# Keeping TensorE's instructions of the three mixers in the order of the kernel's own planner

## The chip, the cores and the metric

The kernel runs on one core of one Trainium2 chip. The metric is the device time of one execution in microseconds (us). The kernel before takes 2852.42 us, the median of 3 runs (2849.89 to 2853.02).

## The reference

Two transformer-like blocks run one after the other on one sequence of 512 positions and 1024 channels, in float32. `x` is `(1, 512, 1024)`.

```python
for l in range(2):                                   # first block
    x = x + 0.5 * swiglu(rmsnorm(x, ffn1_norm[l]), ffn1_w_gu[l], ffn1_w_down[l])
    x = x + hybrid_mixing(rmsnorm(x, mix_norm[l]), w_in[l], ...)
    x = x + 0.5 * swiglu(rmsnorm(x, ffn2_norm[l]), ffn2_w_gu[l], ffn2_w_down[l])
h = rmsnorm(x, final_norm)
u = rmsnorm_2(h, norm_mix)                           # second block
p = u @ w_in
merged = gates[0] * (dilated_mixture_attention(p) @ w_a) \
       + gates[1] * (rwkv7_time_mix(p) @ w_r) + gates[2] * (s5_glu(p) @ w_s)
h = h + merged @ w_out
h = h + swiglu_2(rmsnorm_2(h, norm_ffn), w_gate_up, w_down)
return rmsnorm_2(h, norm_final)
```

`hybrid_mixing` projects its input by `w_in`, runs three branches on slices of the result (latent attention with 6 heads, a moving-average pool, attention with forget gates with 6 heads) and projects their concatenation by `w_out`. The hidden width of each SwiGLU is 2816.

## The kernel before

**Stages.** The program is one straight line: FFN, mixer 1 (layer 0), FFN, FFN, mixer 1 (layer 1), FFN, mixer 2, FFN, last norm. Activations lie feature by position: `x` is eight tiles of 128 channels x 512 positions. Each float32 product is computed from operands that are split into a high and a low part (ScalarE casts the high part, VectorE subtracts for the low one), as three matmuls into one PSUM bank: high x high, high x low, low x high. These are lines L201, L202 and L203 in `mm3`, called a triple here. A projection of 1024 channels to 128 outputs is eight triples, one for each of the eight k, and is called an item.

**The FFNs** are written by plain loops. The last loop of an FFN updates `x[o]` for o = 0 to 7 and calls `after(o)`, which makes the next stage's operand `xin[o]` from `x[o]` (L254, L255) and adds the squares of `x[o]` to `ssum` (L265, L266).

**The mixers** (`mix1` for the first block, `mix2` for the second) are written by a planner, class `Sched`. Every branch is a Python generator, a stream, that yields requests such as `("P", 0.64)` (0.64 us of TensorE), `V6` (0.62 us of VectorE), a wait for an event, or a place in a pool of tiles ("A" and "B" are PSUM, four banks each). The planner keeps a clock for each engine. At every step it finds the engine that can start first, takes among that engine's requests those that can start within `near` of it, picks the one with the lowest priority number, and lets its stream write its instruction into the program. The projections are one stream, `gemm_stream`, with priority 50, the filler: it asks for one triple at a time. Everything else has a lower number and goes first.

At a mixer's start the planner's clocks are set by `FV, FA, FG = 3.0, 2.2, 3.6` (VectorE, ScalarE, GpSimd are free so many us after TensorE), and the norm's stream `prep_end_s`, of priority 0, is ready at `D3` or `D4` = 5.2. Its first instruction is the matmul of `ones` with `ssum` at L285 (in `mix2` a second norm follows, whose matmul of `ones` with `ssum2` is L910). The row scale `rb`, which every evacuation of an item waits for, comes out of that stream. The weights of an item are cast by `load_w` (L393 on ScalarE, 0.97 us in the planner, L395 on VectorE, 1.135 us). The planner of `mix1` has `near` = 0.1 (`N1`) and an event lag of 0.2 (`E1`), that of `mix2` 0.5 (`N2`) and 0.4 (`E2`).

```python
first = min(self.active, key=lambda s: (start(s), s.prio))
t, e = start(first), first.req[0]
near = [x for x in self.active if x.req[0] == e and start(x) <= t + self.near]
s = min(near, key=lambda x: (x.prio + self.load * switch(x), start(x)))
```

`mix2` runs the planner in three parts: "a" (state-space branch, dilated attention, first preparation of the RWKV branch), "u" (RWKV: twelve units, at most four at a time, L1188 to L1341), "g" (gates, merge, `w_out`).

**The order that runs.** The planner decides only the order in which instructions are written. The library's scheduler then works through the whole program with a timing model of its own and may issue, on each engine, a later-written instruction ahead of an earlier one whose inputs its model does not have ready yet; among those that are ready the earlier-written one goes first. `keep_in_program_order` takes that freedom from one instruction: it is put behind the instruction written before it on its engine. The class `InOrder` wraps an engine so that all its instructions are treated so. Before the change it is used for VectorE, ScalarE and GpSimd in `ssm_tables`, and for no TensorE instruction.

Of the kernel before, what the change touches and what calls it, by code (L numbers as in the profile page):

```python
# [42 lines left out]
class Ev:  # L43


    def __init__(self, n=1):
        self.n, self.t, self.waiting = n, 0.0, []
# [7 lines left out]
class Sched:  # L55
# [64 lines left out]
    def run(self, group=0):  # L120
        start = lambda s: max(self.free[s.req[0]], s.ready)
        switch = lambda s: len(s.req) > 3 and s.req[3] != self.table
        while self.live[group]:
            assert self.active, "streams that wait for ever"
# [4 lines that stand above are left out]
            t, dur = start(s), s.req[1]  # L129
            if switch(s):  # L130
                self.table, dur = s.req[3], dur + 1.3
                if self.table in SETS:
                    self.preload(SETS[self.table])
            self.active.remove(s)
            self.free[e] = t + dur
            s.ready = t if len(s.req) > 2 and s.req[2] else t + dur
            s.last = e
            self.step(s)
# [5 lines left out]
class InOrder:  # L144
# [4 lines left out]

    def __getattr__(self, name):  # L150
        return lambda *a, **k: self.tc.keep_in_program_order(getattr(self.engine, name)(*a, **k))


class Kern:
# [220 lines left out]
    def vec(self, name):  # L375
        a, n = self.cols[name]
        return self.vecs[:, a : a + n]
# [1596 lines left out]
    def run(self, cols):  # L1974
        self.cols = cols
        self.x = [None] * NK
        vec = self.vec
        prep = lambda name: lambda o: self.prep_tile(o, vec(name))
        self.consts()
        self.load_x(0, "xT")  # L1980
        w0 = self.wraw("f1gu0", 0, 1024, 4)
        self.load_x(1, "xT")
        self.prep_start()
        self.operands(0, vec("f1n0"))
        w0 = self.wsplit(w0, 1024, 4)
        for k in range(1, NK):
            if k > 1:
                self.load_x(k, "xT")
            self.operands(k, vec("f1n0"))
        first = w0, self.wload("f1gu0", 1, 1024)  # L1990
        self.ident = self.const(self.cp, "ident", (P, P))
        for k in range(NK):
            self.sq_acc(k, self.x[k])
        for l in range(2):
            self.ffn(f"f1gu{l}", f"f1da{l}", f"f1db{l}", 0.25, prep(f"mixn{l}"), None if l else first)
            if self.stop == f"f1_{l}":
                break
            self.mix1(l, prep(f"f2n{l}"))
            if self.stop == f"y{l}":
                break  # L2000
            if self.stop == f"m_{l}":
                break
            last = l == 1
            nxt = (lambda o: self.prep2_tile(o)) if last else prep("f1n1")
            self.ffn(f"f2gu{l}", f"f2da{l}", f"f2db{l}", 0.25, nxt, beside=self.ssm_tables if last else None)
            if self.stop == f"f2_{l}":
                break
        if self.stop and (self.stop[-1] in "01" or self.stop == "b1"):
            self.store_x()
            return  # L2010
        self.mix2(prep("normf2"))
        if self.stop in ("ya", "yr", "ys"):
            return
        if self.stop == "b2m":
            self.store_x()
            return
        self.ffn("f3gu", "f3da", "f3db", 0.5, self.last_tile)
        if self.stop == "b2f":
            self.store_x()
            return  # L2020
        self.last_norm()
# [196 lines left out]
```

## Time and profile before

| | |
|---|---|
| median of 3 runs | 2852.42 us (2849.89 to 2853.02) |
| the profiled execution | 2848.72 us |
| its span, first to last instruction | 2846.8 us |
| TensorE busy (PE) | 2794.3 us, 98% |
| VectorE, ScalarE, GpSimd busy | 58%, 37%, 16% |
| mean granted TensorE clock | 0.994 |

The profiled execution is one run of the program under the hardware profiler. Its own time is 1.9 us more than its span, and 3.7 us less than the median of the runs. PE is TensorE's matmuls; PEld is the loading of their stationary operands, which runs beside them. The ends of matmuls are modelled, so the distance between starts says more of a matmul's cost than its duration does. PEclk is the clock that TensorE was granted as a share of 2.4 GHz: 1.00 or 0.50.

### The profile page before, as it was taken

How to read it: one execution, taken by the hardware profiler on the slowest of the kernel's cores; microseconds unless marked ns; L12 is line 12 of the kernel's file. 1: busy time of each engine (PE TensorE's matmuls, PEld its weight loads, DVE VectorE, ACT ScalarE, POOL GpSimd, SP SyncE). 2: the span in 40 equal slices, each digit the busy share in tenths (PEclk: the TensorE clock that was granted, in tenths of full speed). 3: DMA queues.
4: the chain of work that ended last, by engine and by line, in shares of the span. 5: the costliest groups of instructions: out<-in, count | busy, mean ns of one | idle time of the engine just before them, and what ended most of it. 6: DMA issues, size and time to landing. Idle time of an engine off the chain costs nothing. (4 is left out here: it accounts for less than half of the span.)

```text
span 2846.8 us, 33464 instructions
## 1 busy us (share of the span) xinstructions
PE 2794.3 (98%) x13036; PEld 2221.2 (78%) x13036; DVE 1640.0 (58%) x2544; ACT 1045.9 (37%) x1625; POOL 451.4 (16%) x368
## 2 busy tenths in 40 slices
PE   8999999999999999999999999999999999999998
PEld 6888877688888888887667788886677878788886
DVE  6454566655445554456665755658776756464454
ACT  4222354532223422234454325362324544332223
POOL 2010111020001200012101101124332212210101
PEclk9999999999999999999999999999999999999999
DMA  3223331223232232324122223343232016322322
GB/s 135 96 95 98 104 113 58 69 95 99 98 96 92 95 103 93 100 93 131 54 64 100 97 97 126 104 159 108 77 107 68 34 46 225 104 96 96 97 96 82
DMA packets 92118, 277.45 MB, mean 97 GB/s; under 512 B 11960, under 2 KB 13368, under 8 KB 91960
## 3 DMA queue, kind: packets, MB, share of 16 engines
q1 hardware_dynamic: 91960, 275.32, 29.4%
q8 instruction: 102, 1.67, 0.3%
q14 instruction: 56, 0.46, 0.0%
HBM read 255.87 MB, written 19.40 MB: 97 GB/s over the span
## 5 line engine op out<-in xcount | busy, mean ns | idle before, releaser
L201 PE MATMUL A<-xin,whi 128*128 128x512 f32 x2368 | 943.5, 398 | 6.8 <-ACT whi L192 5.1
L202 PE MATMUL A<-xin,whi 128*128 128x512 f32 x2368 | 933.0, 394 | 1.9 <-DVE xin L255 1.8
L203 PE MATMUL A<-xin,wlo 128*128 128x512 f32 x2368 | 930.2, 393 | 3.6 <-DVE wlo L193 1.9
L192 ACT CAST whi<-wraw 128x1024 fp32r<-128x1024 f32 (+2 forms) x343 | 349.7, 1020 | 1027.0 <-issue 378.1
L193 DVE TENSOR_TENSOR wlo<-wraw,whi 128x1024 fp32r<-128x1024 f32 (+2 forms) x343 | 500.8, 1460 | 86.8 <-ACT whi L192 60.4
L201 PEld LDWEIGHTS A<-xin,whi 128*128 128x128 f32 x2368 | 447.8, 189 | 119.2 <-issue 23.4
L202 PEld LDWEIGHTS A<-xin,whi 128*128 128x128 f32 x2368 | 447.5, 189 | 99.4 <-DVE xin L255 6.1
L203 PEld LDWEIGHTS A<-xin,wlo 128*128 128x128 f32 x2368 | 447.6, 189 | 98.3 <-DVE wlo L193 3.1
L332 POOL TENSOR_TENSOR u<-u,g 128x512 f32<-128x512 f32 x110 | 157.2, 1429 | 1419.0 <-DVE u L330 1145.6
L202 PE MATMUL B<-hl,whi 128*128 128x512 f32 x880 | 343.4, 390 | 1.5 <-DVE hl L217 1.3
L203 PE MATMUL B<-hh,wlo 128*128 128x512 f32 x880 | 342.5, 389 | 0.0
L201 PE MATMUL B<-hh,whi 128*128 128x512 f32 x880 | 342.5, 389 | 0.0
L341 DVE SCALAR_TENSOR_TENSOR x<-B,x 128x512 f32<-128x512 f32 x120 | 83.0, 692 | 307.3 <-PE B L203 307.3
L330 DVE TENSOR_TENSOR u<-A,rb 128x512 f32<-128x512 f32 x110 | 76.0, 691 | 256.2 <-PE A L203 256.2
L393 ACT CAST whi<-wraw 128x1024 fp32r<-128x1024 f32 (+2 forms) x117 | 119.6, 1023 | 214.3 <-PE A L202 133.7
L202 PEld LDWEIGHTS B<-hl,whi 128*128 128x128 f32 x880 | 165.2, 188 | 38.9 <-DVE hl L217 4.9
L201 PEld LDWEIGHTS B<-hh,whi 128*128 128x128 f32 x880 | 165.2, 188 | 34.9
L203 PEld LDWEIGHTS B<-hh,wlo 128*128 128x128 f32 x880 | 165.2, 188 | 34.0
L395 DVE TENSOR_TENSOR wlo<-wraw,whi 128x1024 fp32r<-128x1024 f32 (+2 forms) x117 | 155.3, 1327 | 25.9 <-ACT whi L393 25.3
L326 DVE TENSOR_TENSOR g<-A,rb 128x512 f32<-128x512 f32 x110 | 75.9, 690 | 157.5 <-PE A L203 157.4
L266 POOL TENSOR_TENSOR ssum<-ssum,sq 128x512 f32<-128x512 f32 x54 | 88.7, 1642 | 384.4 <-ACT sq L265 377.6
L216 ACT CAST hh<-u 128x512 fp32r<-128x512 f32 x110 | 68.4, 622 | 159.7 <-POOL u L332 159.7
(462 smaller groups left out, 2816.7 us busy)
## 6 DMA issues: line engine op xcount, KB each, us to landing
wraw<-in_f2gu SPq DMA_DIRECT2D x88, 512.0 KB, 3.3
wraw<-in_f1gu SPq DMA_DIRECT2D x87, 512.0 KB, 3.3
wraw<-in_w_in SPq DMA_DIRECT2D x76, 512.0 KB, 3.4
wraw<-in_f3gu SPq DMA_DIRECT2D x44, 512.0 KB, 3.3
wraw<-in_f1db SPq DMA_DIRECT2D x32, 448.0 KB, 3.2
wraw<-in_f2db SPq DMA_DIRECT2D x32, 448.0 KB, 3.3
wraw<-in_w_out SPq DMA_DIRECT2D x24, 512.0 KB, 3.5
wraw<-in_f1da SPq DMA_DIRECT2D x16, 512.0 KB, 3.3
```

The costliest lines, as they stand in the source:

```text
L192: nc.scalar.copy(hi[:, b], raw[:, b])
L193: nc.vector.tensor_sub(lo[:, b], raw[:, b], hi[:, b])
L201: mm(ps, wh, xh, start=first, stop=False)
L202: mm(ps, wh, xl, start=False, stop=False)
L203: mm(ps, wl, xh, start=False, stop=last)
L266: (nc.vector if k == NK - 1 else nc.gpsimd).tensor_add(self.ssum, self.ssum, sq)
L326: nc.vector.tensor_mul(g, pg, rb)
L330: nc.vector.tensor_mul(u, pu, rb)
L332: nc.gpsimd.tensor_mul(u, u, g)
L341: nc.vector.scalar_tensor_tensor(self.x[o], ps, scale, self.x[o], ALU.mult, ALU.add)
L393: nc.scalar.copy(hi[:, :width], raw[:, :width])
L395: nc.vector.tensor_sub(lo[:, :width], raw[:, :width], hi[:, :width])
```

## The change

During each of the three mixers `self.nc` is replaced by an object whose `tensor` is TensorE wrapped in `InOrder`, and everything else is as it was. Every TensorE instruction that a mixer writes is thereby put behind the TensorE instruction written before it. No instruction is added, removed or altered. The other engines, the DMA queues, and TensorE in the FFNs keep the scheduler's freedom.

```diff
+class Ordered:
+
+
+    def __init__(self, tc):
+        self.nc, self.tensor = tc.nc, InOrder(tc, tc.nc.tensor)
+
+    def __getattr__(self, name):
+        return getattr(self.nc, name)
...
+            self.nc = Ordered(self.tc)
             self.mix1(l, prep(f"f2n{l}"))
+            self.nc = self.tc.nc
...
+        self.nc = Ordered(self.tc)
         self.mix2(prep("normf2"))
+        self.nc = self.tc.nc
```

## Rows read from the trace of the kernel before

**Rows 1.** The page's first line.
```profile
span 2846.8 us, 33464 instructions
```

**Rows 2.** Windows: length; busy (instructions) of PE, PEld, DVE, ACT, POOL; PEclk, DMA share, GB/s.
```profile
375.80:590.00 214.20, 206.81 (x1071) 149.01 (x1070) 138.46 (x367) 107.89 (x228) 26.85 (x28) 1.00 0.23 73
1318.60:1530.00 211.40, 204.03 (x1047) 146.67 (x1046) 135.74 (x364) 105.69 (x225) 24.91 (x27) 0.98 0.23 71
1906.90:2150.00 243.10, 237.56 (x991) 166.97 (x990) 185.75 (x307) 82.35 (x145) 77.65 (x61) 0.98 0.31 105
2150.00:2362.00 212.00, 205.73 (x1429) 162.82 (x1429) 140.58 (x303) 106.95 (x232) 44.08 (x64) 0.99 0.15 51
2362.00:2440.00 78.00, 74.88 (x321) 60.65 (x320) 50.18 (x60) 25.19 (x34) 26.71 (x16) 0.98 0.64 218
```

**Rows 3.** Waits of PE, whole span: line, releaser, total us, times, longest.
```profile
PE B L521 <- DVE s L515: 11.7, 10, 2.1
...
PE B L1258 <- DVE FT L1243: 2.9, 3, 2.1
```

**Rows 4.** Timeline, layer-0 mixer's start: start, us, engine, line, operation, [idle before].
```profile
375.60 0.39 PE L203 MATMUL B<-hh,wlo 128*128 128x512 f32 x1
375.83 0.39 PE L201 MATMUL A<-xin,whi 128*128 128x512 f32 x1
...
376.51 0.39 PE L201 MATMUL A<-xin,whi 128*128 128x512 f32 x1
...
379.64 0.68 DVE L266 TENSOR_TENSOR ssum<-ssum,sq 128x512 f32<-128x512 f32 x1
...
380.38 1.13 PE L285 MATMUL B<-ssum,ones 128*128 128x512 f32 x2
```

**Rows 5.** Timeline of PE, layer-1 mixer's start.
```profile
1318.60 0.39 PE L201 MATMUL A<-xin,whi 128*128 128x512 f32 x1
...
1323.15 0.70 PE L285 MATMUL B<-ssum,ones 128*128 128x512 f32 x1
```

**Rows 6.** Timeline of PE, start of mixer 2.
```profile
1906.93 0.39 PE L201 MATMUL A<-xin,whi 128*128 128x512 f32 x1
...
1911.48 1.13 PE L285 MATMUL B<-ssum,ones 128*128 128x512 f32 x2
...
1914.98 1.02 PE L910 MATMUL B<-ssum,ones 128*128 128x512 f32 x2
...
1930.58 0.39 PE L203 MATMUL A<-xin,wlo 128*128 128x512 f32 x1
1932.29 2.45 PE L1868 MATMUL B<-su,BT 32*128 32x512 f32 x4 [1.32 <-issue]
```

**Rows 7.** Windows around long waits; columns as in Rows 2, PEclk third from last.
```profile
1412.50:1414.70 2.20, 0.10 (x2) 0.06 (x1) 2.20 (x5) 0.48 (x1) 2.14 (x2) 1.00 0.25 15
1414.80:1418.20 3.40, 3.40 (x11) 2.36 (x12) 2.64 (x9) 1.93 (x5) 1.75 (x3) 0.50 0.36 145
1933.70:1940.40 6.70, 6.70 (x16) 4.48 (x15) 5.53 (x8) 0.63 (x1) 5.21 (x5) 0.50 0.28 91
...
2432.10:2435.30 3.20, 3.20 (x7) 2.28 (x8) 1.89 (x3) 1.62 (x2) 0.00 (x0) 0.50 0.17 64
...
470.40:474.00 3.60, 3.60 (x25) 2.50 (x26) 2.71 (x10) 2.05 (x5) 1.82 (x3) 1.00 0.34 125
```

**Rows 8.** Timeline: other matmuls inside a triple, first and last of 88.
```profile
491.59 0.62 PE L569 MATMUL B<-c_ident,w 128*128 128x128 f32 x4
...
505.56 0.39 PE L201 MATMUL A<-qn1h,whi 128*128 128x512 f32 x1
505.70 0.41 DVE L515 TENSOR_SCALAR s<-s,st 128x384 f32<-128x384 f32 x1
...
506.16 0.55 PE L521 MATMUL B<-c_ident,s 128*128 128x128 f32 x3 [0.21 <-DVE s L515]
...
2346.96 1.12 PE L1061 MATMUL B<-sq,c_bones 128*128 128x512 f32 x2
```

## The prediction

> **What bounds the kernel now.** I read the page first, then the windows by stage, then TensorE's waits, then the timeline at the places where those lead. The span is 2846.8 us [rows 1], and TensorE is the bound nearly everywhere: in the five windows that cover the mixers (layer 0, layer 1, and the parts "a", "u", "g" of mixer 2) the length minus PE's busy time is 7.39, 7.37, 5.54, 6.27 and 3.12 us, 29.7 us together [rows 2]. The reader should see that VectorE, the next busiest, has room in each of them. So the change can win at most those 29.7 us and the slow clock that follows some of them, and what it adds in TensorE waits is paid in full unless the same stage has idle time later that takes it up. The longest waits by line are those of the transposes L521 for VectorE's L515, 11.7 us in 10 waits over both layers, and of L1258 for L1243, 2.9 us in 3 [rows 3].
>
> **The change part by part.** It adds and removes no instruction. On the chip a matmul waits for the same operands as before; new is only what stands behind it. Where the scheduler used to let filler triples pass a matmul whose input was late, TensorE now stands still, and with it every triple behind. Nothing moves on SP's or POOL's queue by the edit itself. VectorE, ScalarE and GpSimd are left to the scheduler and have room [rows 2], so I cost their reordering at nothing; without that room the delay of an engine would come back as lateness of the matmuls that I count below.
>
> *The start of each first-block mixer.* In the planner the first item's weights are cast from 2.2 to 3.17 us on ScalarE and from 3.30 to 4.435 us on VectorE, so with the lag of 0.2 the first triple is taken at 4.635 and ends at 5.275. The norm's matmul L285 is ready at 5.2 and has priority 0: it comes second. The written order is one triple, L285, the rest. In the trace the first triple starts at 375.83, the second at 376.51 (a triple is 0.68 us), and L285 only at 380.38, right after VectorE's last sum of squares ends at 380.32 [rows 4]: six triples and a matmul were let past it, because the weights had in fact been cast during the FFN. Kept in order, TensorE stands from 376.51 to 380.38, 3.87 us. Layer 1 repeats it: 1318.60 + 0.68 = 1319.28 to 1323.15, 3.87 us [rows 5]. Nothing hides it, since L285 waits for the FFN's own last tile. It isn't won back by `rb` either, which comes no earlier; the items come later by so much, and the attention that uses up the mixer hangs on items. I take all of it, 2 x 3.87 = 7.7 us; the ends are nothing (the later idle 7.4 us takes it up) and 7.7.
>
> *The start of mixer 2.* The first triple could be taken at 4.835 (lag 0.4), but L285 at 5.2 lies within the 0.5 of `near` and wins: it is written ahead of every triple. The trace bears that out by the next matmul of that stream: the planner puts L910 at the first free place from 12.34 on, and L285's end at 6.06 plus ten triples of 0.64 is 12.46; in the trace thirty matmuls of the filler, ten whole triples, run from 1906.93 until L910 at 1914.98, nineteen of them ahead of L285 [rows 6]. So the order written is L285, ten triples, L910. Kept, TensorE stands from 1906.93 to 1911.48, 4.55 us. Part of it comes back: before, four items filled the four banks "A" by 1930.58 and TensorE then waited 1.32 us for `rb` [rows 6]; 4.55 us later that wait is gone. Net 4.55 - 1.32 = 3.2 us.
>
> *The clock.* After the wait of 2.1 us before 1414.6 the granted clock was 0.50, the 1.2 GHz level, for 3.4 us, and after the longest in the mixers for as long from 2432.1 on; in the stretch from 1933.7 it was 0.50 for 6.7 us; after a like wait of 2.1 us before 470.3 it stayed at 1.00 [rows 7]. A stretch of 3.4 us at half speed does 1.7 us of work, so it costs 1.7 us. The starts' waits are nearly twice as long as the one that slowed it, so I count 1.7 us for each first-block mixer, 3.4 us; for mixer 2 a slow stretch at the start stands against the 6.7 us that no longer follow a wait, and I count nothing. The Trainium skill (TensorE: Matmul & The Clock Gate, Part 1: The HAM clock gate) says that half speed is TensorE's default and that idleness sends it back there. By that alone each of the three starts would pay 1.7 us, 5.1 instead of 3.4; the stretch from 470.4 shows that not every wait of this size does.
>
> The starts sum to 7.7 + 3.2 + 3.4 = 14.3 us.
>
> *Inside the mixers.* Where a matmul of a branch stands between two matmuls of a triple, the scheduler has put it back: the planner never splits a triple, so it was written ahead of it. There are 88 such places beside the three L285, 10 in each first-block mixer, 22 in part "a" and 46 in part "u"; the first and the last of them stand in the rows [rows 8]. Kept in order, TensorE would wait where the triple began until the operand was there. At 505.56 a triple begins, L515 ends at 505.70 + 0.41 = 506.11, L521 starts at 506.16 after 0.21 us of idleness that was there already: 0.39 us more [rows 8]. The same difference, with 0.06 us from the writer's end to the matmul, over all 88 and with those ready in time at 0, sums to 2.6 + 2.6 + 5.6 + 11.0 = 21.7 us. Matmuls put back by whole triples stand on a boundary and don't show; if lateness is spread evenly over a triple, a third does, and the upper end is 1.5 x 21.7 = 32 us. The lower end is about 0: a wait for one branch lets the others' VectorE and ScalarE work catch up, so that the next is not late any more. I take half the upper end, 16 us, since several streams are in flight in every part.
>
> Sum: 14.3 + 16 = 30.3 us, 2848.7 + 30.3 = 2879 us for the profiled execution; the median of the runs lay 3.7 us above it, so 2883 us.
>
> **The rivals.** *Only the starts cost* (waits inside the mixers share one another's time, or fall into idleness that was there): 2852.4 + 14.3 = 2867 us. For it: 29.7 us of idle time are there to be filled [rows 2]. Against it: that idleness sits in a few long waits, and the 88 places are spread.
>
> *Lateness piles up* in part "u", where 46 of 87 passages from a triple to another matmul are inside a triple, so that its order is far from the written one. At one triple of 0.68 us for each of the 87 it costs 59 us: 2852.4 + 14.3 + 59 = 2926 us.
>
> *Faster: the scheduler's order is itself what causes the waits.* L521's waits of both layers (11.7 us) [rows 3] and all idle time of "a" and "u" (5.54 + 6.27 us) [rows 2] would go, and with them half of the slow stretches from 1414.8 and 1933.7 and of two like the former in mixer 2 (1.7 + 3.4 + 3.4 us) [rows 7]: 32 us. It decides from 14.3 us on, where the starts are paid; in full it gives 2852.4 + 14.3 - 32 = 2835 us. For it: some matmuls were issued some 2 us ahead of their operand, which a better plan would not do. Against it: the scheduler only lets later-written work pass, so the written order has that matmul no later relative to the triples that passed it.
>
> *No effect*: the written order is the one that already runs, 2852 us. Against it speak L910's ten triples.
>
> **How the numbers follow.** The forecast of 2883 us gets 0.38 (its own range 2868 to 2900: the starts with 0 to 32 us), only the starts 0.24, piling up 0.12, faster 0.17, no effect 0.09. The range is 2842 to 2926: below it lies most of the faster case, above it half of the piling up, under 0.2 together. A measurement of this kernel can tell about 0.2%, 5.7 us, from no change. Slower holds the first three, 0.74; the same holds no effect and a little of the faster case, 0.10; faster 0.16.
>
> **What would show it.** In the profile after, each first-block mixer begins with one triple, a PE wait of about 3.8 us for VectorE's `ssum`, then L285; mixer 2 begins with a wait of about 4.5 us and L285, and L910 follows ten triples later. PEclk shows 0.50 behind these. No triple has another matmul inside it, and PE's waits by line grow by many short ones for L515, L477, L482, L1243 and the copies at L441. The prediction is wrong if L285 still comes after several triples, if the windows of "a" and "u" are no longer than now, or if L521's waits shrink by more than the starts add.

## The result, and the profile after

The kernel with the change took 2903.16 us (median of 4 runs, 2902.27 to 2903.88), the kernel before on the same chip 2852.72 us (4 runs, 2849.89 to 2854.03). The ratio is 1.0182, with a 95% interval of 1.0168 to 1.0197: slower by 50.4 us. The forecast was slower, by 30.3 us.

The profiled execution took 2902.65 us against 2848.72, 53.9 us more. Lines in the mixers have moved by 10, and all their TensorE instructions now carry the line of the wrapper, L151; the triples of the FFNs are L211 to L213. The page's first line, and its busy times:

```profile
span 2900.9 us, 33474 instructions
...
PE 2812.7 (97%) x13036; PEld 2232.6 (77%) x13036; DVE 1645.9 (57%) x2544; ACT 1043.0 (36%) x1623; POOL 455.4 (16%) x368
```

TensorE runs the same 13036 instructions, is busy 18.4 us longer (2812.7 - 2794.3) and the span grew by 54.1: the rest is idle time. These are the windows of the same stages, with the columns of [rows 2]. Each ends behind the last wait of its stage; the counts of instructions show that the ends are not at the same instruction, so what can be compared is the idle time:

```profile
376.27:592.70 216.43, 200.80 (x1029) 144.30 (x1028) 134.60 (x361) 103.32 (x222) 23.71 (x26) 0.98 0.22 69
1331.10:1545.20 214.10, 198.86 (x1013) 142.04 (x1013) 132.94 (x360) 102.57 (x221) 21.94 (x25) 0.97 0.22 68
1930.20:2186.70 256.50, 242.82 (x995) 170.51 (x994) 187.26 (x309) 82.29 (x145) 81.74 (x61) 0.97 0.30 99
2186.70:2399.70 213.00, 196.36 (x1358) 153.29 (x1358) 137.27 (x295) 99.08 (x223) 42.35 (x64) 0.98 0.13 43
2399.70:2493.00 93.30, 89.97 (x385) 72.89 (x384) 55.90 (x66) 30.21 (x41) 26.73 (x16) 0.98 0.59 200
```

Length minus PE's busy time is 15.63, 15.24, 13.68, 16.64 and 3.33 us, 64.5 together, where [rows 2] gave 29.7. The stages before "g" gained 8.2, 7.9, 8.1 and 10.4 us of idle time, "g" 0.2. The first three hold a mixer's start each; without the waits there (3.70, 3.70 and 4.38 us, below) 4.5, 4.2 and 3.8 us are left, so inside the mixers "u", the stage with the most places in triples, lost by far the most.

Added up over all of TensorE's records, idleness grew by 35.6 us. In the mixers the granted clock was 0.50 in thirteen stretches of 3.4 us and one of 6.8 us, where before there were five and one: eight more, each worth 1.7 us, are 13.6 us of work not done. (At the end of the program it was low for 2.8 us longer, where TensorE has hardly any work.) 4.7 us is left over. These three make the 53.9. The mean granted clock is 0.989 in all four runs of the change; in the 19 runs of the kernel before beside e9 to e11 it is 0.993 to 0.997.

Whom TensorE waits for, over the whole span (columns as in [rows 3]):

```profile
PE B L151 <- DVE s L525: 14.2, 16, 2.1
PE B L151 <- DVE ssum L276: 11.8, 3, 4.4
PE B L151 <- DVE FT L1253: 10.7, 13, 3.1
...
PE A L151 <- ACT sT L451: 4.9, 12, 0.7
...
PE B L151 <- issue: 1.8, 1, 1.8
```

L525 is L515 of before, and L1253 is L1243. The waits for `s` grew from 11.7 us in 10 to 14.2 in 16, those for `FT` from 2.9 us in 3 (1.6 more in one by another matmul's line) to 10.7 in 13. New is the wait for `ssum`, 11.8 us in 3: the three starts, which answer to [rows 4 to 6]. Timeline of PE:

```profile
376.27 0.61 PE L151 MATMUL A<-xin,whi 128*128 128x512 f32 x2
376.73 0.39 PE L151 MATMUL A<-xin,wlo 128*128 128x512 f32 x1
380.82 2.07 PE L151 MATMUL B<-ssum,ones 128*128 128x512 f32 x2 [3.70 <-DVE ssum L276]
...
1331.61 0.39 PE L151 MATMUL A<-xin,wlo 128*128 128x512 f32 x1
1335.70 1.51 PE L151 MATMUL B<-ssum,ones 128*128 128x512 f32 x2 [3.70 <-DVE ssum L276]
...
1929.87 0.39 PE L213 MATMUL B<-hh,wlo 128*128 128x512 f32 x1
1934.63 2.08 PE L151 MATMUL B<-ssum,ones 128*128 128x512 f32 x2 [4.38 <-DVE ssum L276]
...
1945.22 1.02 PE L151 MATMUL B<-ssum,ones 128*128 128x512 f32 x2
...
1955.38 0.39 PE L151 MATMUL A<-xin,wlo 128*128 128x512 f32 x1
1957.56 0.66 PE L151 MATMUL B<-su,BT 32*128 32x512 f32 x1 [1.79 <-issue]
```

One triple, a wait of 3.70 us, the norm's matmul; in mixer 2 a wait of 4.38 us with no triple ahead, and the second norm's matmul after exactly thirty matmuls. The view counts a wait from the modelled end of the matmul before; by the distance of starts, as the forecast counted, less 0.23 us for that matmul, the three are 3.86, 3.86 and 4.53 us. In none of the 88 places of [rows 8] does another matmul stand inside a triple any more. The last two rows were not foreseen: the wait before the matmul on `su` was 1.32 us in [rows 6] and should have gone; it is 1.79 us.

The clock behind waits (columns as in [rows 7]): the start of layer 0, two places later in that mixer, the start of mixer 2, and part "g".

```profile
380.60:384.00 3.40, 3.18 (x6) 1.86 (x7) 0.85 (x2) 0.48 (x2) 0.00 (x0) 0.50 0.44 126
476.20:479.60 3.40, 3.40 (x16) 2.36 (x16) 2.43 (x10) 2.11 (x5) 1.50 (x3) 0.51 0.33 119
513.70:517.10 3.40, 3.15 (x9) 2.35 (x9) 2.10 (x6) 2.01 (x6) 0.00 (x0) 0.50 0.45 126
1933.60:1940.30 6.70, 5.67 (x11) 3.85 (x12) 2.43 (x5) 3.27 (x5) 0.00 (x0) 0.50 0.92 308
2486.70:2490.10 3.40, 3.40 (x10) 2.66 (x9) 2.39 (x3) 1.78 (x3) 0.00 (x0) 0.51 0.21 40
```

The first and the fourth are the starts (mixer 2 had a stretch as long before). The fifth was there before too. The second and third lie behind waits inside the mixers of 2.10 and 1.54 us. The second is not the change's alone: before, layer 1 had the like at 1414.8 [rows 7], and two of the runs below (e3, e9) that leave the layer-0 mixer as it was have it there. The third is new: it stands in both first-block mixers of the four traces in which these are kept in order with the planner's lag as it was (this one, e2, e6, e11), and in no other trace.

### The profile page after: what moved, and what is told of

Read it like the earlier page. It is cut to its first block, busy times and chain, and to the rows that moved or that the text cites. A ratio compares the mean times of both kernels' runs of the same rounds, so it can differ in the third digit from the quotient of the medians.

```text
span 2900.9 us, 33474 instructions
## 1 busy us (share of the span) xinstructions
PE 2812.7 (97%) x13036; PEld 2232.6 (77%) x13036; DVE 1645.9 (57%) x2544; ACT 1043.0 (36%) x1623; POOL 455.4 (16%) x368
## 5 line engine op out<-in xcount | busy, mean ns | idle before, releaser
L211 PE MATMUL A<-xin,whi 128*128 128x512 f32 x1760 | 688.4, 391 | 7.3 <-ACT whi L202 5.1
L212 PE MATMUL A<-xin,whi 128*128 128x512 f32 x1760 | 686.9, 390 | 2.1 <-DVE xin L265 2.0
L213 PE MATMUL A<-xin,wlo 128*128 128x512 f32 x1760 | 686.0, 390 | 1.9 <-DVE wlo L203 1.9
L151 PE MATMUL A<-xin,whi 128*128 128x512 f32 x1216 | 401.1, 411 | 0.0
L211 PEld LDWEIGHTS A<-xin,whi 128*128 128x128 f32 x1760 | 331.0, 188 | 77.3 <-ACT whi L202 5.1
L213 PEld LDWEIGHTS A<-xin,wlo 128*128 128x128 f32 x1760 | 331.0, 188 | 71.8 <-DVE wlo L203 3.1
L211 PE MATMUL B<-hh,whi 128*128 128x512 f32 x880 | 342.5, 389 | 0.0
L213 PE MATMUL B<-hh,wlo 128*128 128x512 f32 x880 | 342.4, 389 | 0.0
L151 PEld LDWEIGHTS A<-xin,whi 128*128 128x128 f32 x1216 | 225.1, 193 | 68.9 <-issue 28.8
L151 PE MATMUL A<-xin,wlo 128*128 128x512 f32 x608 | 241.3, 397 | 1.7 <-DVE wlo L405 1.7
L211 PEld LDWEIGHTS B<-hh,whi 128*128 128x128 f32 x880 | 165.1, 188 | 34.9
L213 PEld LDWEIGHTS B<-hh,wlo 128*128 128x128 f32 x880 | 165.2, 188 | 34.2
L405 DVE TENSOR_TENSOR wlo<-wraw,whi 128x1024 fp32r<-128x1024 f32 (+2 forms) x117 | 155.3, 1327 | 21.7 <-ACT whi L403 20.7
```

The costliest lines, as they stand in the source:

```text
L211: mm(ps, wh, xh, start=first, stop=False)
L212: mm(ps, wh, xl, start=False, stop=False)
L213: mm(ps, wl, xh, start=False, stop=last)
L405: nc.vector.tensor_sub(lo[:, :width], raw[:, :width], hi[:, :width])
```

## The experiments

All ratios are to the kernel before on the same chip. "Kept" means that TensorE's instructions are kept in the written order there; elsewhere the scheduler is free.

**e1: only the starts kept** (the first eight TensorE requests from L285 on; then the wrapper hands out the free engine).

```diff
     @property
     def tensor(self):
+        if self.left is not None:
+            self.left -= 1
+            self.on = self.left >= 0
+        return self.pin if self.on else self.nc.tensor
...
+            if nc.left is None:
+                nc.left = 8
```

> TensorE is kept in the planner's order only from each mixer's start until eight triples after the norm's matmul of ones and ssum; the rest of each mixer is left to the scheduler. Theory (the starts are paid in full, with the slow clock behind them): waits for ssum of 3.7 + 3.7 + 4.4 us, less 0.2 us that the kernel before waited there, and 1.7 us of slow clock at each first-block mixer, about 15 us: 2868 us. Rival (the later idle time of the mixers takes the starts' waits up): 2853 to 2858 us.

Measured 2869.19 us, ratio 1.0068 (1.0051 to 1.0085): 18.7 us more. The starts are paid in full, and the rival (2853 to 2858 us) falls; the forecast's 14.3 us lies just below the interval's lower end of 14.5. The same three waits stand in its trace:

```profile
PE B L151 <- DVE ssum L283: 11.8, 3, 4.4
```

**e2: all kept, and the planner counts no time for the casts of each mixer's first item.**

```diff
-    def load_w(self, name, idx, width, out):
+    def load_w(self, name, idx, width, out, cast=True):
...
-        yield ("A", 0.12 + width * 0.00083)
+        if cast:
+            yield ("A", 0.12 + width * 0.00083)
...
-                w = self.load_w(*items[i][:2], width(i), ws)
+                w = self.load_w(*items[i][:2], width(i), ws, i > 0)
```

> The changed kernel, but the planner counts no time for the cast of each mixer's first item, which in the traces is done during the FFN; so it writes eight triples ahead of the norm's matmul in the first-block mixers and seven in mixer 2. Theory: in the first-block mixers the wait for ssum and its slow clock go, 2 x (3.7 + 1.7) = 10.8 us; in mixer 2 the wait only moves from ssum to the next matmul that hangs on rb (the one that reads su), since as many triples stand ahead of that as in the changed kernel: 2892 us. Rival (all three starts are won back, about 15.5 us): 2888 us or less. Rival (the starts cost nothing net): 2903 us.

Measured 2890.61 us, ratio 1.0141 (1.0125 to 1.0156), as the theory had it. The plan now writes triples ahead of the norm's matmul, so none of the three starts waits for `ssum`. But in mixer 2 the time is given back at the next matmul of that chain, which waits for `rb` as before. Timeline of PE in mixer 2:

```profile
1916.23 0.61 PE L151 MATMUL A<-xin,whi 128*128 128x512 f32 x2
...
1920.99 1.02 PE L151 MATMUL B<-ssum,ones 128*128 128x512 f32 x2
...
1942.73 2.04 PE L151 MATMUL B<-su,BT 32*128 32x512 f32 x2 [8.28 <-issue]
```

4.38 + 1.79 = 6.2 us of waits became one of 8.28 us.

**e3: only part "u" kept** (the first-block mixers are not wrapped; in mixer 2 the wrapper starts switched off, and is on during the planner's run of "u").

```diff
...
+        nc.on = True
         sch.run("u")
+        nc.on = False
...
```

> TensorE is kept in the planner's order only in part u of mixer 2 (the RWKV units). Theory (lateness piles up): in the kernel before, the last matmuls of the units stand up to 69 filler matmuls later than written, 69 x 0.227 = 15.7 us; kept in order all of that is waited for: about 2869 us. Rival (the waits of one unit give time to the others, as half of the places inside triples, 11 us, had it): 2858 to 2861 us. Rival (the loss of mixer 2 comes from part a): 2853 us.

Measured 2868.06 us, ratio 1.0064 (1.0049 to 1.0079): 17.5 us more against the 15.7 us of the theory. That figure came from the order in which the two kernels' instructions are written and issued: at the end of "u" the scheduler had let 69 filler matmuls pass, 69 x 0.227 us. The put-back adds up over the stage and is paid in full. Not all of it shows as waits: from the start of "u" to the next FFN the trace is 18.4 us longer than before, of which 9.8 us are more idle time of TensorE and 3.4 us more slow clock; 5.2 us lie in neither.

**e4 and e5: the planner counts 0.5 us instead of 0.2 us from another engine's end to the TensorE instruction that uses its result**, with all kept (e4) and with nothing kept (e5).

```diff
-TO = dict(P=0.2, V=0.13, A=0.13, G=0.13)
+TO = dict(P=0.5, V=0.13, A=0.13, G=0.13)
```

> The changed kernel, but the planner counts 0.5 us instead of 0.2 us from another engine's end to a TensorE instruction that hangs on it. Theory (the waits inside the mixers come from matmuls written for the very moment at which the planner has their operand): most waits of 0.2 to 0.5 us go, about half of the 38 us lost inside the mixers, 2884 us (2878 to 2890). Rival (the waits come from few places where the plan is wrong by a microsecond or more, or from the order of the streams): 2898 to 2908 us.

Measured 2894.53 us, ratio 1.0159 (1.0144 to 1.0175), between the two theories. In its windows of "a" and "u" the idle time is 265.20 - 245.90 = 19.3 us (13.7 after the change alone) and 8.95 us (16.6):

```profile
1928.40:2193.60 265.20, 245.90 (x994) 172.21 (x994) 185.44 (x306) 83.22 (x148) 79.28 (x61) 0.95 0.29 96
2193.70:2401.50 207.80, 198.85 (x1391) 161.16 (x1391) 142.08 (x313) 99.19 (x212) 41.87 (x63) 0.98 0.14 48
```

"u" gained 7.7 us and "a" gave 5.6 of them back, with a clock of 0.95. The run told nothing clear of the cause, because it changed every plan; e9 to e11 repeat it for "u" alone.

> The kernel before (nothing kept in order) with the planner's 0.5 us instead of 0.2 us: what that constant does without the change, the control for the run with both. Theory (the gain of the run with both comes from fewer waits of kept matmuls): no gain here, 2850 to 2858 us. Rival (the constant makes the plan better for the whole kernel): 2842 to 2846 us, and what the run with both gained has nothing to do with the change.

Measured 2855.28 us, ratio 1.0022 (1.0012 to 1.0031). With the order free the lag wins nothing, it costs 5.5 us: e4's gain exists only where the written order binds.

**e6: all kept except the starts and "u".**

> TensorE is kept in the planner's order in the mixers except at their starts (until eight triples after the norm's matmul) and in part u of mixer 2. Theory (the parts add up): the changed kernel lost 50 us, the starts alone 19, part u alone 17, so 14 us are left for the attention of the first-block mixers and part a of mixer 2: 2866 us. Rival (waits at the start bring about the waits further in, by the slow clock or by weights that come late): 2853 to 2859 us. Rival (the parts take time from one another, and each alone costs more): 2872 us or more.

Measured 2873.08 us, ratio 1.0083 (1.0068 to 1.0098): 23.3 us, where the parts should have left 50.4 - 18.7 - 17.5 = 14.2. The theory of 2866 us falls, and the time lies where the last rival puts it, by which each part alone costs more. e1, e3 and e6 make 18.7 + 17.5 + 23.3 = 59.5 us, and all together 50.4. One row shows where a part is counted twice, the matmul on `su` again:

```profile
1943.04 2.04 PE L151 MATMUL B<-su,BT 32*128 32x512 f32 x2 [6.72 <-issue]
```

With the start free the triples that passed L285 are used up early, and the kept matmul on `su` waits 6.72 us, 4.9 more than the 1.79 with everything kept. 59.5 - 4.9 = 54.6 us; the 4 us that remain are within the three intervals (each 4 to 5 us to either side).

**e7: "u" with TensorE and VectorE kept.**

```diff
+        self.pinv = InOrder(tc, tc.nc.vector)
...
+    @property
+    def vector(self):
+        return self.pinv if self.on else self.nc.vector
```

> As the run with part u alone, and in that part VectorE too is kept in the planner's order; TensorE's order is the same to the instruction. Theory (TensorE waits in u because VectorE's instructions stand in another order than the plan's): most of the 10 us of new waits go, 2856 to 2861 us. Rival (they are in the plan's order or near it, and take longer than planned, such as those beside GpSimd): 2866 to 2880 us.

Measured 2864.66 us, ratio 1.0050 (1.0035 to 1.0065): between the two, and nearer to the rival. Idle time of "u" fell only from 214.70 - 198.84 = 15.86 us in e3 to 13.60:

```profile
2151.20:2359.80 208.60, 195.00 (x1358) 152.27 (x1358) 138.28 (x295) 99.41 (x223) 42.84 (x63) 0.99 0.13 44
```

VectorE's free order is at most a small part of the cause: 14.9 us against e3's 17.5, with intervals that overlap. My first explanation, that the results come late because the scheduler puts other work ahead of them on VectorE, falls as the main one. No run kept ScalarE's or GpSimd's order.

**e8: the plan of e2 with nothing kept.**

> The kernel before (nothing kept in order), but the planner counts no time for the cast of each mixer's first item. Theory (the scheduler makes good such errors of the plan, as it lets filler pass a late matmul): 2848 to 2856 us. Rival (a better plan helps it too): 2840 to 2846 us.

Measured 2848.45 us, ratio 0.9997 (0.9987 to 1.0006). The free scheduler makes such an error of the plan good by itself.

**e9 and e10: "u" alone kept, as in e3, with the lag of 0.5 us (e9) or 1.0 us (e10) in "u" alone.** The edit of e9, shown against e3:

```diff
...
         nc.on = True
+        TO["P"] = 0.5
         sch.run("u")
+        TO["P"] = 0.2
         nc.on = False
...
```

> Part "u" alone is kept in order, as in e3_u_only, and in that part alone the planner counts 0.5 us instead of 0.2 us from another engine's end to the TensorE instruction that uses its result. Theory (the written order is too optimistic about when VectorE's and ScalarE's results are there, so matmuls stand too early among the triples and TensorE waits): with 0.3 us more at each step most of the put-back is in the written order already; the idle time of "u" falls from 15.9 us towards the 9 us that e4_lag_half showed, and the time from 2868 us to 2858 us (2855 to 2862). Rival (the waits come from the order in which the other engines work, which a lag for TensorE does not touch): 2865 to 2870 us, idle time of "u" 13 us or more.

> The same with 1.0 us instead of 0.2 us, in part "u" alone. Theory (the plan is too optimistic): the idle time of "u" falls to the 6 to 7 us that it had with the order free, and the time to 2855 us (2851 to 2860), a little above the kernel before, since a branch then takes longer in the plan. Rival (the other engines' order): 2865 to 2870 us. A second rival (a lag that is too long makes the branches the bound of the plan, and the filler runs out): above 2870 us, with the idle time at the end of "u".

Measured 2855.31 us, ratio 1.0021 (1.0011 to 1.0031), and 2852.29 us, ratio 1.0009 (1.0000 to 1.0019). The cost of keeping "u" in order goes from 17.5 to 6.5 to 3.5 us by the lag alone, the last not told apart from none. TensorE's waits for `FT` in "u", in e3, e9 and e10:

```profile
PE B L151 <- DVE FT L1260: 10.0, 13, 3.1
```

```profile
PE B L151 <- DVE FT L1260: 5.3, 6, 2.9
```

```profile
PE B L151 <- DVE FT L1260: 3.8, 2, 3.6
```

The written order was too optimistic about these results, and that is what "u" paid for. One detail of the expectations missed: the idle time of "u" is 10.2 us in e9, where some 9 were expected, and 10.6 us in e10, not 6 to 7. In e10 the stage holds more triples and its boundary lies later (227.1 us long, with part "g", up to the first matmul of the next FFN, 97.7), so "u" and "g" together are the fair measure: 321.0 us before, 339.4 in e3, 327.4 in e9, 324.8 in e10. With the order free the lag of 0.5 us leaves them at 320.0 us (e5), so what e9 won is not a plan that is better in itself.

**e11: all kept, with e2's plan and the lag of 0.5 us in "u".**

> All three mixers kept in order, with two changes to the plan: no time counted for the casts of each mixer's first item (e2_first_item_ready, 2890.6 us) and the lag of 0.5 us in part "u". Theory: the two gains add up, so 2881 us (2876 to 2885). Rival (the lag moves the waits elsewhere, as in part "a" of e4_lag_half): 2887 to 2893 us.

Measured 2877.35 us, ratio 1.0093 (1.0078 to 1.0108): the gains add up, and nearly half of the change's loss is gone. The wait before `su` is still there, 8.3 us, and so is the cost inside the other parts. No version with the order kept beats the kernel before.

## Why the prediction was right in direction and short in size

**What bounds the kernel.** Right. What was added to TensorE's waits was paid: of the 29.7 us of idle time that were there, nothing was won by the kept order.

**The starts, 14.3 us.** Right as a mechanism, in each part but one. By the distance of starts the waits were 3.86, 3.86 and 4.53 us (3.87, 3.87 and 4.55 forecast); the clock was low for 3.4 us, 1.7 us of work, at each first-block mixer, and at mixer 2 for no longer than before. (Of the six triples and a matmul that stood ahead of L285, one triple was written there, so five triples and a matmul were let past it; the sum does not use that count.)

The step that failed is "4.55 us later that wait is gone". The matmul on `su` hangs on the `rb` of the second norm, and the kept order made that later in itself. The second norm's matmul started 3.50 us after the first norm's before [rows 6]; kept behind ten triples, the first three of them at the clock of 0.50, it started 10.59 us after it. VectorE in mixer 2, before and after: the first norm's `rb`, and the product of it with the second norm's sum.

```profile
1918.43 0.69 DVE L468 SCALAR_TENSOR_TENSOR rb<-sq,sq 128x512 f32<-128x512 f32 x1
...
1919.22 0.69 DVE L912 TENSOR_TENSOR sq<-B,rb 128x512 f32<-128x512 f32 x1
```

```profile
1941.59 0.69 DVE L478 SCALAR_TENSOR_TENSOR rb<-sq,sq 128x512 f32<-128x512 f32 x1
...
1946.72 0.68 DVE L922 TENSOR_TENSOR sq<-B,rb 128x512 f32<-128x512 f32 x1
```

The product followed 0.1 us after the first `rb` before, and 4.4 us after it now. The matmul on `su` came 22.93 us after the first norm's matmul (20.81 before), with 24 triples written ahead of it where the scheduler had let 32 pass. So its wait grew by 0.47 us in place of going.

Read from the trace the starts are 11.8 + 3.4 = 15.2 us. In e1, where that matmul is free, the wait does go (0.25 us is left); the 18.7 us that e1 took all the same go with more slow clock: in its trace the layer-0 mixer has 13.7 us at 0.50, where the kernel before has none. Not all of that need come from the starts, since e3 has 6.8 us at 0.50 in the same mixer without any edit to it; but the mean clock is 0.989 to 0.992 in the four runs of e1 and 0.994 to 0.997 in the seven of the kernel before beside them.

**Inside the mixers, 16 us.** This is the term that was mis-sized: 53.9 - 15.2 = 38.7 us, above even the upper end of 32. It has two faults. First, "I take half the upper end, since several streams are in flight in every part": a wait for one stream did not let the others catch up enough. Idle time outside the starts grew by 35.6 - 11.8 = 23.8 us, 23.0 of it in the mixers. That is more than two thirds of the 32 us that spread lateness gave, and close to the plain sum over the 88 places, 21.7 us. In part that closeness is luck: by stage the sum had 2.6, 2.6, 5.6 and 11.0 us, and 4.5, 4.2, 3.8 and 10.4 came. The reason for the cost is that the plan has results at TensorE too early, step after step, and that the delays of a stage add up. e9 and e10 show it for "u": more time per step in the plan, and nearly all of the cost is gone. For the other stages it is argued, not shown. That a triple is 0.64 us in the plan and 0.68 us on the chip, and an operation of VectorE on 128 x 512 0.62 and 0.68 us [rows 4], may add to it; no run changed these numbers. Second, the clock was priced at the three starts alone. The mixers have more slow stretches inside too, 13.6 - 3.4 = 10.2 us of work lost; which of them the added waits brought is borne out for one place only, that of the stretch at 513.7. The remaining 4.7 us of the 38.7 I cannot place.

The Trainium skill (TensorE: Matmul & The Clock Gate, Part 1: The HAM clock gate) says that half speed is the default and that idleness leads back to it. At the starts the trace agrees: behind all three long waits the clock is 0.50, from 380.6, 1336.3 and 1933.6 on. For the short ones the rule alone does not size the cost, and in one place the clock fell with no idleness before it, as the last section shows.

**The engines left free, nothing.** Nearly right: e7 puts VectorE's order at some 3 us in "u" (17.5 against 14.9 us, with intervals that overlap, so it may be nothing). One passage shows how it can work, DVE, POOL and PE in "u" after the change:

```profile
2252.90 1.21 DVE L405 TENSOR_TENSOR wlo<-wraw,whi 128x1024 fp32r<-128x1024 f32 x1
...
2254.04 0.68 DVE L1130 SCALAR_TENSOR_TENSOR AR<-w,w 128x512 f32<-128x512 f32 x1
...
2254.64 0.41 DVE L1253 TENSOR_TENSOR FT<-B,c_mlev 128x256 f32<-128x256 f32 x1
...
2254.80 1.27 POOL L1132 TENSOR_TENSOR w<-w,w 128x512 f32<-128x512 f32 x1 [3.62 <-DVE AR L1130]
2254.98 1.64 DVE L1046 SCALAR_TENSOR_TENSOR w<-w,vecs,zb 128x512 f32<-128x512 f32 x1
...
2255.11 0.71 PE L151 MATMUL B<-C,FT 128*128 128x128 f32 x4 [1.79 <-DVE FT L1253]
```

A weight cast and an operation of another stream's preparation run ahead of `FT` on VectorE, and TensorE stands still for 1.79 us with triples ready behind.

**The rivals.** "Only the starts cost" fails by e3 and e6. "Lateness piles up" was right in kind and too large in size: one triple for each of 87 passages, 59 us, where 23 triples, 15.7 us, had piled up by the end of "u". "Faster" fails: L521's waits grew from 11.7 to 14.2 us instead of going. "No effect" fails with the starts.

What is not settled: how the cost inside the two first-block mixers and part "a" divides among too-short promises and the other engines' order (e4's longer lag made "a" worse, and no run took it alone), and how much of the slow clock the added waits brought. What a slow stretch costs by itself the layer-0 mixer of e3 and e9 shows, which is TensorE's work of before in the same order: with 7.4 us of idle time in all three it took 221.5 us before, and 224.3 and 224.4 us with two stretches of 3.4 us at 0.50 in e3 and in e9, so some 1.5 us for each instead of the 1.7 us reckoned. The eight more of the change would be 12 us by that.

## What to carry to other kernels

An order that a planner writes is only as good as its durations; a scheduler that may let ready work pass made such an error of the plan good at no cost that could be measured (e8), and taking that freedom away makes an error a wait of the engine that bounds the kernel (e2, e9, e10). Count the put-back at the end of a stage, in instructions that were let past, and price it in full rather than halving it for overlap, as held for "u" here. Follow a chain through a kept order too: a matmul that is kept behind filler delays what hangs on its result. Then leave room for the clock, and take its cost from the mean of several runs, since single stretches come and go. If an order must be kept, put the measured lateness into the plan first: 0.8 us more per step took the cost of "u" from 17.5 to 3.5 us.

## What the runs showed of the hardware that was not expected

- The clock fell behind waits much shorter than those of the starts, and not always. Behind the wait of 1.54 us that ends at 512.81 (another of 0.59 us follows) it was 0.50 for 3.4 us from 513.7; behind the wait of 2.10 us that ends at 475.80, 0.50 from 476.2. The same wait of 2.1 us in the same stage before left it at 1.00 [rows 7].
- TensorE's instructions and waits do not decide it alone. e3 and e10 leave the layer-0 mixer as it was, and TensorE runs it in the same order with the same wait of 2.10 us (it ends at 471.33 in e3, at 470.31 in e10). Behind it the clock was 0.50 in e3 and 1.00 in e10 (columns as in [rows 7]):

```profile
471.20:474.60 3.40, 3.27 (x9) 2.35 (x9) 2.72 (x11) 1.62 (x4) 2.04 (x3) 0.50 0.43 149
```

```profile
470.30:473.70 3.40, 3.39 (x24) 2.45 (x24) 2.70 (x10) 1.75 (x4) 1.92 (x3) 1.00 0.42 142
```

- Nor is a wait needed. In layer 1 before, TensorE was busy in all of the 7.00 us up to 1343.00, at 1.00, and then the clock was 0.50 for 3.4 us; in layer 0, at the same place of the program, it stayed at 1.00 (398.3 to 401.7), and in e3 it fell there too, at 399.5.

```profile
1343.10:1346.50 3.40, 3.40 (x9) 2.65 (x9) 1.56 (x4) 1.04 (x1) 0.00 (x0) 0.50 0.33 130
1336.00:1343.00 7.00, 7.00 (x29) 4.69 (x28) 5.50 (x6) 3.26 (x5) 1.59 (x2) 1.00 0.29 77
```

- What tells these cases apart no run shows. So the slow stretches of one execution cannot all be put down to what the kernel does there.
- In the passage above L1046, an operation of VectorE on 128 x 512, took 1.64 us, while L1130 of the same kind and size took 0.68 us. GpSimd's L1132 had begun 0.18 us ahead of L1046 and ended at 2256.07; L1046 ended at 2256.62, 0.55 us later. The Trainium skill (SBUF — State Buffer, SBUF: two separate sides) says that VectorE with two SBUF inputs and GpSimd share a port, and that the second to start is blocked until the first has ended. These rows agree with it, and so do two operations a little earlier: L476 (from 2249.25, 1.02 us) and L478 (from 2250.53, 1.19 us) each ended 0.54 us after the GpSimd operation that had begun before it (the spans of GpSimd are rough). The planner counts 0.62 us for such an operation whatever runs beside it.
